# Moving a third of a depthwise convolution's taps to ScalarE and GpSimd, with all memory keys from split weights

## The chip, the cores and the metric

The kernel runs on one core of one Trainium2 chip. The metric is the device time of one execution in microseconds (us), as the median of several runs. TensorE (PE in the profile) does the matrix products, VectorE (DVE) and ScalarE (ACT) the elementwise work, GpSimd (POOL) the same at need, and SyncE (SP) issues the loads.

## The reference, cut to what matters

Two transformer blocks follow each other on 256 tokens of width 1024. The change lies in the first block. It normalises the tokens, projects them with `w_in` to queries, keys, values and the two halves of a gated convolution, runs an attention on the former and the convolution on the latter, and joins both with `w_out`. After that each token attends to a second sequence `mem` of 256 rows, which is normalised by itself and projected to keys `xk` and values `xv`.

```python
u = a * jax.nn.sigmoid(g)
u = lax.conv_general_dilated(u, conv_w.reshape(CONV_WIDTH, 1, C), ...) + conv_b
u = layernorm(u, ln_g, ln_b)
...
mn = rmsnorm(mem, norm_mem_g[l])
xk = (mn @ w_xk[l]).reshape(B, M, XATT_HEADS, XATT_HEAD_DIM)
```

The convolution is depthwise: 512 channels, 31 taps along the tokens, each channel with its own 31 weights. Everything is float32, to float32's accuracy.

## The kernel before, in words

Activations lie feature-major: a tile holds 128 features on the partitions and 256 tokens along the row. Weights come in one packed stream of blocks of 128x1024 (8 pieces of 128x128), each loaded by SP into a `raw` buffer. For the fast matrix format each block is split in two: ScalarE rounds it to a high part (`whi`, line 286) and VectorE subtracts to get the low part (`wlo`, line 287). Activations are split alike. A product of a piece is then three matmuls (`mm3`, line 484): high by high, high by low, low by high. There are four buffers each for raw, high and low blocks.

The stage that the change touches runs in this order in the program: the gate of the convolution (`ag`), the values (`v`), the queries and keys (`qk`, eight outputs from line 689) with the attention's steps between them, the keys of the memory (`xk`, lines 714 to 722), the layer norm of the convolution (726 to 750), the values of the memory (`xv`, 752), and `w_out` in two halves (line 763): half 0 takes the attention's four chunks `mh[0..3]`, half 1 the convolution's four chunks `mh[4..7]`. A scheduler turns the program's order into one fixed queue per engine: it takes what is ready by its own estimate of the times, the earlier in the program first. So an engine's queue can hold work of a later line before that of an earlier one, and once built the queue is strict.

The convolution (`conv_steps`, lines 589 to 599) keeps one sum `cacc[c]` for each of four groups of 128 channels. Tap 0 is written by ScalarE with the bias, and the taps 1 to 30 are added by VectorE, one `scalar_tensor_tensor` each (`upad` shifted, times a column of weights, plus the sum), 120 in all. `conv_hook(n)` emits n steps after a product is done.

The memory (lines 695 to 724): a `Norm` object makes from each of eight chunks a high and a low half (`parts`, line 453) and the square (`square`, line 459). The halves live in the tiles `xhi0..3` and `xlo0..3`, of which there is one buffer each, and in which the halves of the tokens lie as long as `qk` reads them. With `pe=True` the squares are summed by one float32 matmul against ones for each chunk (line 463), otherwise by VectorE adds (line 468) and one such matmul at the end (line 475). The first four outputs of `xk` are made by plain float32 matmuls from unsplit weights (`W.plain`, which holds the raw buffer until the matmuls are done) and from `mf`, a copy of the chunk times the gain, which ScalarE writes (line 702). The other four use split weights.

Of the kernel before, what the change touches and what calls it, by code (L numbers as in the profile page):

```python
# [11 lines left out]
AF = mybir.ActivationFunctionType  # L12
ALU = mybir.AluOpType
# [3 lines left out]
P = 128  # L17
T = 256
D = 1024
KD = D // P  # L20
# [11 lines left out]
CW = 31  # L32
# [271 lines left out]
def emit(tc, xT, memT, wts, params, consts, out, tap=None):  # L304
    nc = tc.nc
# [3 lines left out]
    def pool(name, bufs=1, space=None, st=None):  # L309
        kw = {} if space is None else {"space": space}  # L310
        return (st or es).enter_context(tc.tile_pool(name=name, bufs=bufs, **kw))
# [5 lines left out]
    psA = pool("psA", 3, PSUM)  # L317
# [5 lines left out]
    def nm(s):  # L323
        uid[0] += 1
        return f"{s}_{uid[0]}"

    def tl(p, shape, tag, dt=F32, bufs=None):
        kw = {} if bufs is None else {"bufs": bufs}
        return p.tile(shape, dt, tag=tag, name=nm(tag), **kw)

    def bank(which=None):
        return tl(which or psD, [P, 512], "bank")

    V, S, G, PE = nc.vector, nc.scalar, nc.gpsimd, nc.tensor

    def mm(o, l, r, start=True, stop=True, **kw):
        PE.matmul(o, l, r, start=start, stop=stop, **kw)  # L337
# [24 lines left out]
    def tt(o, a, b, op, eng=None):  # L362
        (eng or V).tensor_tensor(out=o, in0=a, in1=b, op=op)  # L363

    def stt(o, a, s, b, op0, op1):
        V.scalar_tensor_tensor(out=o, in0=a, scalar=s, in1=b, op0=op0, op1=op1)  # L366
# [16 lines left out]
    def pr(name, a=0, n=None):  # L383
        o, w = poff[name]
        return pm[:, o + a:o + (w if n is None else a + n)]
# [7 lines left out]
    W = _Stream(nc, wts, [wraw], whi, wlo)  # L393
# [4 lines left out]
    ps = bank()  # L398
# [26 lines left out]
    def both(x):  # L425
        hi = x[0]
        return bass.AP(hi.tensor, hi.offset, [list(hi.ap[0]), [1, 2 * T]])
# [56 lines left out]
    def mm3(ps, wh, wl, x, first, last):  # L484
        mm(ps, wh, x[0], first, False)
        mm(ps, wh, x[1], False, False)
        mm(ps, wl, x[0], False, last)


    def dense_s(sec, hl, nk, evac, nts, hook=None, it=None, wide=False):  # L490
        it = it or W.take(sec)
        for nt in nts:
            pw = bank(psA)
            ps = pw[:, :T]
            for k in range(nk):
                wh, wl = next(it)
                if wide:
                    mm(pw, wh, both(hl[k]), k == 0, False)
                    mm(ps, wl, hl[k][0], False, k == nk - 1)
                else:  # L500
                    mm3(ps, wh, wl, hl[k], k == 0, k == nk - 1)
            if wide:
                evac(nt, ps, pw[:, T:])
            else:
                evac(nt, ps)
            if hook:
                hook()
        return it
# [27 lines left out]
    with ExitStack() as st:  # L536
        at = pool("b1", 1, st=st)
# [17 lines left out]
        upad = [tl(at, [P, T + CW - 1], f"up{c}") for c in range(4)]  # L555
# [30 lines left out]

        cacc = [tl(at, [P, T], f"cacc{c}") for c in range(4)]

        def conv_steps():
            for c in range(4):  # L590
                a = cacc[c]
                for i in range(CW):
                    wcol = pr("cw", c * CW + i, 1)
                    src = upad[c][:, i:i + T]
                    if i == 0:
                        S.activation(a, src, AF.Identity, bias=pr("cb", c, 1), scale=wcol)
                    else:
                        stt(a, src, wcol, a, ALU.mult, ALU.add)
                    yield

        conv = conv_steps()

        def conv_hook(n=4):
            for _ in range(n):
                if next(conv, "end") == "end":
                    return

        n1.cols()
        vtok = [tl(at, [P, 512], f"vtok{t}") for t in range(2)]

        def ev_v(j, t, ps):
            S.activation(vtok[t], ps, AF.Copy, scale=n1.col(t))

        dense_m("v", n1.hl, KD, 512, ev_v, 1, lambda: conv_hook(4))
        for a, b in ((0, 1024), (1024, NC1)):
            nc.sync.dma_start(out=cs1[0][:, a:b], in_=consts[:, a:b])
# [25 lines left out]
        def att_scores(c):  # L642
            pss = [bank(), bank()]
            for q in range(2):
                for j in range(2):
                    mm(pss[j][:, q * T:(q + 1) * T], qt[c][hf[j], q * P:(q + 1) * P], kt[c][hf[j], :])
            for j in range(2):
                ps = pss[j]
                p = tl(at, [P, 2, T], "prob", bufs=4)
                mx = tl(at, [P, 4], "mx", bufs=4)  # L650
                for q in range(2):
                    ttr(p[:, q, :], ps[:, q * T:(q + 1) * T], cst("lm", q * T, T), ALU.add, ALU.min, BIG, mx[:, q:q + 1])
                for q in range(2):
                    actv(p[:, q, :], p[:, q, :], AF.Exp, bias=mx[:, q:q + 1], scale=-1.0, accum_out=mx[:, 2 + q:3 + q])
                V.reciprocal(mx[:, 2:4], mx[:, 2:4])
                for q in range(2):
                    S.activation(p[:, q, :], p[:, q, :], AF.Copy, scale=mx[:, 2 + q:3 + q])
                aps[2 * c + j] = p

        def att_turn(c):  # L660
            for kt_ in range(2):
                ps = bank()
                for j in range(2):
                    for q in range(2):
                        PE.transpose(ps[:, j * T + q * P:j * T + (q + 1) * P], aps[2 * c + j][:, q, kt_ * P:(kt_ + 1) * P], ident)
                apts[c, kt_] = tl(at, [P, 512], "pt", bufs=4)
                S.copy(apts[c, kt_], ps)

        def att_out(c):
            po = bank(psF)  # L670
            for kt_ in range(2):
                for j in range(2):
                    mm(po[hf[j], :T], vtok[kt_][:, c * P + 64 * j:c * P + 64 * j + 64], apts[c, kt_][:, j * T:(j + 1) * T],
                       kt_ == 0, kt_ == 1)
            split(po[:, :T], *mh[c])

        def att_steps():
            att_scores(0)
            yield
            for c in range(4):  # L680
                if c < 3:
                    att_scores(c + 1)
                    yield
                att_turn(c)
                att_out(c)
                yield

        itq, att = W.take("qk"), att_steps()
        for nt in range(8):
            dense_s("qk", n1.hl, KD, ev_qk, (nt,), conv_hook, it=itq)  # L690
            if nt in (1, 3, 4, 5, 6, 7):
                next(att)


        nmem = Norm(lambda c: pr("memg", c, 1), pe=True)
        mf = []
        for c in range(KD):
            mt = tl(at, [P, T], "mem", bufs=2)
            nc.sync.dma_start(out=mt, in_=memT[:, c * T:(c + 1) * T])
            nmem.chunk(c, mt)  # L700
            mf.append(tl(at, [P, T], f"mf{c}"))
            S.activation(mf[c], mt, AF.Copy, scale=pr("memg", c, 1))
        nmem.finish()
        nmem.cols()
        xk = [tl(kv, [P, T], f"xk{c}") for c in range(8)]
        xv = [tl(kv, [P, D], f"xv{t}") for t in range(2)]

        def ev_xk(nt, ps):
            tt(xk[nt], ps, nmem.rstd, ALU.mult)
# [1 line left out]
        def ev_xv(j, t, ps):  # L711
            S.activation(xv[t][:, j * 512:(j + 1) * 512], ps, AF.Copy, scale=nmem.col(t))

        itp = W.plain("xkp")
        for nt in range(4):
            ps = bank(psA)[:, :T]
            for k in range(KD):
                mm(ps, next(itp), mf[k], k == 0, k == KD - 1)
            ev_xk(nt, ps)
            next(att, None)  # L720
            conv_hook(10)
        dense_s("xk", nmem.hl, KD, ev_xk, range(4, 8), lambda: conv_hook(10))
        conv_hook(200)


        ps = bank()
# [9 lines left out]
        ps = bank()  # L736
# [31 lines left out]
    for b in range(4):  # L768
        ps = bank((psF, psD)[b // 2])
# [27 lines left out]
    with ExitStack() as st:  # L797
        at = pool("b1x", 1, st=st)
# [7 lines left out]
        for hd in range(XH):  # L806
            dense_s("xq", nx.hl, KD, ev_xq, (2 * hd, 2 * hd + 1), it=itq)
            ps = bank()
# [6 lines left out]
            p = tl(at, [P, 2, T], "prob", bufs=3)  # L815
# [30 lines left out]
    with ExitStack() as st:  # L846
        at = pool("b1m", 1, st=st)
# [39 lines left out]
    ps = bank()  # L887
# [506 lines left out]
    with ExitStack() as st:  # L1394
        at = pool("ff", 1, st=st)
# [113 lines left out]
    ps = bank(psF)  # L1509
# [22 lines left out]
    ps = bank(psF)  # L1532
# [134 lines left out]
```

## Time and profile before

| | us |
|---|---|
| median of 3 runs | 1341.27 (1338.58 to 1342.76) |
| profiled execution | 1341.65 |
| its span | 1339.9 |

The span is the time from the first to the last instruction of the one execution that was profiled; 1.75 us of its time lie around the span. Busy time of an engine counts the time in which one of its instructions runs; a pipelined successor starts a little before the record of the one in front of it ends, so the step from start to start is the price of one more instruction, and the recorded duration is an upper bound for it. A float32 matmul leaves two records. "Idle before" and the views of waits name what ended an engine's idle time. The granted clock is 1.00 at TensorE's 2.4 GHz.

### The profile page before, as it was taken

How to read it: one execution, taken by the hardware profiler on the slowest of the kernel's cores; microseconds unless marked ns; L12 is line 12 of the kernel's file. 1: busy time of each engine (PE TensorE's matmuls, PEld its weight loads, DVE VectorE, ACT ScalarE, POOL GpSimd, SP SyncE). 2: the span in 40 equal slices, each digit the busy share in tenths (PEclk: the TensorE clock that was granted, in tenths of full speed). 3: DMA queues.
4: the chain of work that ended last, by engine and by line, in shares of the span. 5: the costliest groups of instructions: out<-in, count | busy, mean ns of one | idle time of the engine just before them, and what ended most of it. 6: DMA issues, size and time to landing. Idle time of an engine off the chain costs nothing.

```text
span 1339.9 us, 22099 instructions
## 1 busy us (share of the span) xinstructions
PE 1317.6 (98%) x8095; PEld 1134.1 (85%) x8095; DVE 1059.0 (79%) x1765; ACT 871.5 (65%) x1438; POOL 75.5 (6%) x94
## 2 busy tenths in 40 slices
PE   9999999999999999999999999999999999999997
PEld 8878998888889897888888989888888788778775
DVE  7999857887668866877766886579888888887885
ACT  7663745655556847655554674668787777777774
POOL 0000000000000000022210000000101001001000
PEclk9999999999999999999999999999999999999999
DMA  8525534655554442555555444268989999999995
GB/s 291 192 83 201 169 126 136 201 188 189 189 188 150 123 131 74 172 190 188 187 184 187 158 120 138 87 204 309 373 312 377 363 378 340 358 384 332 362 394 178
DMA packets 94918, 298.27 MB, mean 223 GB/s; under 512 B 16016, under 2 KB 21456, under 8 KB 94800
## 3 DMA queue, kind: packets, MB, share of 16 engines
q1 hardware_dynamic: 92032, 291.52, 62.1%
q0 software_dynamic: 2624, 5.24, 2.0%
q8 instruction: 65, 1.06, 0.3%
q14 instruction: 53, 0.43, 0.1%
q10 hardware_dynamic: 144, 0.00, 0.0%
HBM read 289.72 MB, written 7.01 MB: 221 GB/s over the span
## 4 chain that ended last, share of the span: by engine, by line
PE 59%; issue 20%; DMA 11%; DVE 7%; ACT 2%; SPq 0%; POOL 0%; POOLq 0%; DVEq 0%; ACTq 0%
PE bank L337 58%; DMA out_dram<-yl,ix 9%; DVE wlo L287 2%; DVE cacc L366 2%; DMA raw<-in_w_dram 1%; ACT whi L286 1%; DMA pws<-dd 1%; DMA dd<-At 0%; DVE w L363 0%; DVE mid L366 0%; ACT prob L357 0%; DMA zc<-dz 0%; DVE rot L363 0%; PE bank L1127 0%; PE bank L825 0%
## 5 line engine op out<-in xcount | busy, mean ns | idle before, releaser
L287 DVE TENSOR_TENSOR wlo<-raw,whi 128x1024 fp32r<-128x1024 f32 (+1 forms) x544 | 644.4, 1210 | 153.5 <-ACT whi L286 151.0
L286 ACT CAST whi<-raw 128x1024 fp32r<-128x1024 f32 (+1 forms) x544 | 549.2, 1039 | 275.8 <-PE bank L337 159.1
L337 PE MATMUL bank<-xhi,whi 128*128 128x256 f32 (+1 forms) x864 | 240.1, 329 | 0.0
L337 PE MATMUL bank<-xlo,whi 128*128 128x256 f32 (+1 forms) x864 | 238.3, 327 | 0.4 <-DVE xlo L366 0.3
L337 PE MATMUL bank<-xhi,wlo 128*128 128x256 f32 x584 | 166.0, 284 | 1.6 <-DVE wlo L287 1.6
L337 PE MATMUL bank<-xlo,wlo 128*128 128x256 f32 x584 | 167.2, 286 | 0.0
L337 PEld LDWEIGHTS bank<-xhi,whi 128*128 128x128 f32 x864 | 146.4, 191 | 18.1 <-issue 2.4
L337 PEld LDWEIGHTS bank<-xlo,whi 128*128 128x128 f32 x864 | 145.8, 191 | 16.2 <-DVE xlo L366 0.7
L337 PE MATMUL bank<-whi,xeh 128*128 128x512 f32 x384 | 152.8, 398 | 0.0
L337 PE MATMUL bank<-whi,xel 128*128 128x512 f32 x384 | 152.0, 396 | 0.0
L337 PE MATMUL bank<-wlo,xeh 128*128 128x512 f32 x384 | 151.7, 395 | 0.0
L337 PEld LDWEIGHTS bank<-xhi,wlo 128*128 128x128 f32 x584 | 111.3, 191 | 3.0 <-DVE wlo L287 2.2
L337 PEld LDWEIGHTS bank<-xlo,wlo 128*128 128x128 f32 x584 | 111.3, 191 | 1.3 <-issue 0.7
L337 PE MATMUL bank<-whi,mid 128*128 128x512 f32 x256 | 91.0, 395 | 0.0
L337 PEld LDWEIGHTS bank<-wlo,xeh 128*128 128x128 f32 x384 | 72.0, 187 | 22.1 <-DVE wlo L287 2.2
L337 PE MATMUL bank<-u,whi 128*128 128x512 f32 x256 | 89.9, 393 | 0.0
L337 PEld LDWEIGHTS bank<-whi,xel 128*128 128x128 f32 x384 | 72.1, 188 | 16.7
L337 PEld LDWEIGHTS bank<-whi,xeh 128*128 128x128 f32 x384 | 72.1, 188 | 14.6
L337 PE MATMUL bank<-u,wlo 128*128 128x256 f32 x256 | 72.4, 283 | 0.0
L337 PE MATMUL bank<-f,whi 128*128 128x512 f32 x176 | 61.8, 393 | 0.0
L337 PEld LDWEIGHTS bank<-u,whi 128*128 128x128 f32 x256 | 48.1, 188 | 11.1
L337 PEld LDWEIGHTS bank<-whi,mid 128*128 128x128 f32 x256 | 47.5, 188 | 10.2
(397 smaller groups left out, 2113.9 us busy)
## 6 DMA issues: line engine op xcount, KB each, us to landing
raw<-in_w_dram SPq DMA_DIRECT2D x532, 512.0 KB, 4.9
raw<-in_w_dram SPq DMA_DIRECT2D x8, 384.0 KB, 3.7
raw<-in_w_dram SPq DMA_DIRECT2D x8, 256.0 KB, 4.9
dd<-At SPq DMA_DIRECT2D x6, 256.0 KB, 2.8
h<-in_x_dram SPq DMA_DIRECT2D x8, 128.0 KB, 4.8
mem<-in_mem_dram SPq DMA_DIRECT2D x8, 128.0 KB, 2.4
out_dram<-xhi POOLq DMA_DIRECT2D x4, 256.0 KB, 3.9
cs<-in_c_dram SPq DMA_DIRECT2D x1, 931.0 KB, 7.0
```

What stands on the lines that cost most here:

```text
L286: nc.scalar.copy(hi[:, s:e], raw[:, s:e])
L287: nc.vector.tensor_tensor(out=lo[:, s:e], in0=raw[:, s:e], in1=hi[:, s:e].bitcast(F32), op=ALU.subtract)
L337: PE.matmul(o, l, r, start=start, stop=stop, **kw)
L366: V.scalar_tensor_tensor(out=o, in0=a, scalar=s, in1=b, op0=op0, op1=op1)
```

## The change

VectorE keeps the sums of groups 0 and 2 and the taps 0 to 15 of group 3. All 31 taps of group 1, and the taps 16 to 30 of group 3 in a sum of their own (`chalf`), become products that ScalarE writes to a tile `tap` (six buffers) and that GpSimd adds up. VectorE adds `chalf` at the end. Each call of `conv_hook` also emits up to three of these side steps. The memory's chunks are loaded and split within the `qk` loop, with four buffers in place of two, their squares are summed by VectorE, `mf` is gone, and the first four outputs of `xk` use split weights as the others do.

```diff
+        chalf = tl(at, [P, T], "chalf")
+
+        def product(a, c, i, bias=False):
+            wcol = pr("cw", c * CW + i, 1)
+            src = upad[c][:, i:i + T]
+            if bias:
+                S.activation(a, src, AF.Identity, bias=pr("cb", c, 1), scale=wcol)
+            else:
+                S.activation(a, src, AF.Copy, scale=wcol)
+
+        def side_steps():
+            for a, c, i0 in ((cacc[1], 1, 0), (chalf, 3, 16)):
+                product(a, c, i0, c == 1)
+                for i in range(i0 + 1, CW):
+                    p = tl(at, [P, T], "tap", bufs=6)
+                    product(p, c, i)
+                    tt(a, a, p, ALU.add, G)
+                    yield
+
+        side = side_steps()
+
         def conv_steps():
-            for c in range(4):
-                a = cacc[c]
-                for i in range(CW):
-                    wcol = pr("cw", c * CW + i, 1)
-                    src = upad[c][:, i:i + T]
-                    if i == 0:
-                        S.activation(a, src, AF.Identity, bias=pr("cb", c, 1), scale=wcol)
-                    else:
-                        stt(a, src, wcol, a, ALU.mult, ALU.add)
+            for c, n in ((0, CW), (2, CW), (3, 16)):
+                product(cacc[c], c, 0, True)
+                for i in range(1, n):
+                    stt(cacc[c], upad[c][:, i:i + T], pr("cw", c * CW + i, 1), cacc[c], ALU.mult, ALU.add)
                     yield
+            for _ in side:
+                pass
+            tt(cacc[3], cacc[3], chalf, ALU.add)
...
             for _ in range(n):
                 if next(conv, "end") == "end":
                     return
+            for _ in range(3):
+                next(side, None)
...
+        nmem = Norm(lambda c: pr("memg", c, 1))
         itq, att = W.take("qk"), att_steps()
         for nt in range(8):
             dense_s("qk", n1.hl, KD, ev_qk, (nt,), conv_hook, it=itq)
             if nt in (1, 3, 4, 5, 6, 7):
                 next(att)
-        nmem = Norm(lambda c: pr("memg", c, 1), pe=True)
-        mf = []
-        for c in range(KD):
-            mt = tl(at, [P, T], "mem", bufs=2)
-            nc.sync.dma_start(out=mt, in_=memT[:, c * T:(c + 1) * T])
-            nmem.chunk(c, mt)
-            mf.append(tl(at, [P, T], f"mf{c}"))
-            S.activation(mf[c], mt, AF.Copy, scale=pr("memg", c, 1))
+            if 2 <= nt < 6:
+                for c in (2 * nt - 4, 2 * nt - 3):
+                    mt = tl(at, [P, T], "mem", bufs=4)
+                    nc.sync.dma_start(out=mt, in_=memT[:, c * T:(c + 1) * T])
+                    nmem.chunk(c, mt)
...
-        itp = W.plain("xkp")
-        for nt in range(4):
-            ps = bank(psA)[:, :T]
-            for k in range(KD):
-                mm(ps, next(itp), mf[k], k == 0, k == KD - 1)
-            ev_xk(nt, ps)
+        def xk_hook():
             next(att, None)
-            conv_hook(10)
-        dense_s("xk", nmem.hl, KD, ev_xk, range(4, 8), lambda: conv_hook(10))
+            conv_hook(6)
+
+        dense_s("xkp", nmem.hl, KD, ev_xk, range(4), xk_hook)
+        dense_s("xk", nmem.hl, KD, ev_xk, range(4, 8), xk_hook)
         conv_hook(200)
```

## Rows read from the trace of the kernel before

**Rows 1.** The page's first part: busy time of each engine over the span.
```profile
PE 1317.6 (98%) x8095; PEld 1134.1 (85%) x8095; DVE 1059.0 (79%) x1765; ACT 871.5 (65%) x1438; POOL 75.5 (6%) x94
```

**Rows 2.** Busy time by stretch; columns: length, PE, PEld, DVE, ACT, POOL, PE clock, DMA, GB/s.
```profile
24.50:74.50 50.00, 49.27 (x357) 43.98 (x355) 49.05 (x132) 31.90 (x67) 2.08 (x2) 1.00 0.59 203
74.50:110.00 35.50, 34.07 (x206) 27.84 (x202) 33.88 (x89) 22.12 (x48) 0.00 (x0) 1.00 0.38 126
110.00:136.00 26.00, 23.63 (x106) 19.07 (x104) 24.16 (x41) 8.70 (x10) 0.00 (x0) 0.93 0.58 191
136.00:154.00 18.00, 18.00 (x125) 16.82 (x126) 13.98 (x26) 13.57 (x24) 0.00 (x0) 1.00 0.42 138
...
150.00:420.00 270.00, 269.34 (x1643) 240.48 (x1642) 196.18 (x337) 148.47 (x258) 1.39 (x8) 1.00 0.54 175
```

**Rows 3.** What PE waited for between 15 and 200 us: total, times, longest.
```profile
PE bank L337 <- DVE wlo L287: 1.6, 2, 0.8
PE bank L337 <- DVE cacc L366: 1.2, 1, 1.2
```

**Rows 4.** Busy time by stretch, as above, of the split keys and the stretch behind the waits.
```profile
100.00:109.90 9.90, 9.90 (x80) 9.77 (x79) 9.40 (x21) 5.47 (x6) 0.00 (x0) 1.00 0.64 212
114.50:118.70 4.20, 4.20 (x22) 4.20 (x23) 2.99 (x4) 0.00 (x0) 0.00 (x0) 0.59 0.58 192
```

**Rows 5.** The timeline of PE around 96 to 100 us: start, length of the merged piece.
```profile
96.40 4.15 PE L337 MATMUL bank<-mf,raw 128*128 128x256 f32 x18
100.20 0.47 PE L337 MATMUL bank<-xhi,whi 128*128 128x256 f32 x1
```

**Rows 6.** Groups of instructions between 15 and 150 us, on PE: busy, mean ns, idle before.
```profile
L337 PE MATMUL bank<-mf,raw 128*128 128x256 f32 x64 | 15.9, 382 | 0.6 <-ACT mf L702 0.6
L337 PE MATMUL bank<-sq,ones 128*128 128x256 f32 x16 | 5.0, 403 | 0.5 <-ACT sq L461 0.5
```

**Rows 7.** The timeline of DVE between 107 and 115 us.
```profile
107.73 2.85 DVE L366 SCALAR_TENSOR_TENSOR cacc<-up,pm,cacc 128x256 f32<-128x256 f32 x7
110.50 0.42 DVE L363 TENSOR_TENSOR xk<-bank,rstd 128x256 f32<-128x256 f32 x1
...
113.20 1.22 DVE L287 TENSOR_TENSOR wlo<-raw,whi 128x1024 fp32r<-128x1024 f32 x1
114.34 0.48 DVE L366 SCALAR_TENSOR_TENSOR cacc<-up,pm,cacc 128x256 f32<-128x256 f32 x1
```

**Rows 8.** Groups of instructions between 24.5 and 136 us, on ACT.
```profile
L286 ACT CAST whi<-raw 128x1024 fp32r<-128x1024 f32 x26 | 27.3, 1049 | 30.5 <-DMA raw<-in_w_dram 15.2 <-PE bank L337 12.7 <-DVE cacc L366 1.7
...
L702 ACT ACTIVATE mf<-mem,pm 128x256 f32<-128x256 f32 x8 | 4.0, 494 | 0.0
```

**Rows 9.** GpSimd's adds elsewhere in this kernel: ns min/median/max, first and last start.
```profile
L363 POOL TENSOR_TENSOR fg<-fg,rstd x22: 733/1464/1470, 562.3 to 680.9; 128x256 f32<-128x256 f32 x22
```

**Rows 10.** The timeline of DVE, and that of POOL, around 50 us.
```profile
49.98 0.63 DVE L363 TENSOR_TENSOR rot<-rot,cs 128x256 f32<-128x256 f32 x1
...
50.94 0.41 DVE L363 TENSOR_TENSOR kt<-rot,rot 128x256 f32<-128x256 f32 x1
...
49.50 0.84 POOL L757 CAST br<-brf 128x786 fp32r<-128x786 f32 x1 [4.05 <-DMA brf<-in_c_dram]
```

**Rows 11.** One group of DVE (ns min/median/max), and the POOL copies beside its last three.
```profile
L363 DVE TENSOR_TENSOR X<-mid,eg x6: 277/280/767, 493.0 to 824.0; 128x128 f32<-128x128 f32 x6
...
822.04 1.70 POOL L1280 COPY Xf<-Xt 64x768 f32<-64x768 f32 x2 [79.15 <-ACT Xt L1273]
```

**Rows 12.** `w_out`: its inputs' last halves, and its products on PE (first and last start).
```profile
L337 PE MATMUL bank<-mh,whi x128: 281/282/285, 142.2 to 165.0; 128*128 128x256 f32 x128
...
L363 DVE TENSOR_TENSOR mh<-rot,mh x4: 418/421/426, 144.7 to 150.3; 128x256 fp32r<-128x256 f32 x4
```

**Rows 13.** The memory's chunks: ACT's timeline at 79 us, and SP's own waits.
```profile
79.45 0.51 ACT L456 ACTIVATE xhi<-mem,pm 128x256 fp32r<-128x256 f32 x1 [4.19 <-DMA mem<-in_mem_dram]
...
SPq L699 <- DVE xhi L366: 14.5, 3, 11.5
```

## The prediction

> **What bounds the kernel now.** I read the busy table first: PE is busy for 1317.6 of 1339.9 us [rows 1], so only what shortens PE's queue, or what PE waits for, can count. Then the stretches. The change lies between 24.5 and 154 us, and there two engines are full, not one: over the first three stretches PE is busy for 49.27 + 34.07 + 23.63 = 107.0 us of 111.5, and DVE for 49.05 + 33.88 + 24.16 = 107.1 [rows 2]. ACT has room: 31.90 + 22.12 + 8.70 = 62.7. The row for 150 to 420 us shows PE busy for 269.34 of 270, so a shift at 154 us should be carried to the end, and none is made good there.
>
> The waits show how DVE reaches PE: twice a low half of weights came late (1.6 us), once a convolution sum (1.2) [rows 3]. After them the granted clock fell to a mean of 0.59 for 4.2 us, between the levels of 1.2 and 2.4 GHz [rows 4]. Set against full clock that is 4.2 x 0.41 = 1.7 us.
>
> **The change, part by part. PE.** The plain keys are 32 matmuls of two records, 64, and the squares 16 records [rows 6]. Eighteen such records take 100.20 - 96.40 = 3.80 us, 0.211 each [rows 5]; the mean duration of 0.38 is pipelined and isn't the price. So 80 x 0.211 = 16.9 us go. In come 32 x 3 = 96 split matmuls at 9.90 / 80 = 0.124 us [rows 4], 11.9 us, and one float32 matmul on the summed squares, 2 x 0.211 = 0.4. PE's balance: 16.9 - 11.9 - 0.4 = **4.6 us less**.
>
> **DVE.** There were 4 x 30 = 120 taps, and 30 + 30 + 15 = 75 stay; 45 go. Seven taps take 110.50 - 107.73 = 2.77 us, 0.396 each [rows 7]: 17.8 us less. In come four more low halves, at 114.34 - 113.20 = 1.14 us [rows 7], 4.6 us, and seven adds of squares and one of `chalf`, at 0.42 as a 128x256 operation of two tensors has it [rows 7], 3.4 us. Without more, DVE has 17.8 - 8.0 = 9.8 us less.
>
> **GpSimd and what it costs DVE.** GpSimd adds 30 + 14 = 44 products. Its adds of this shape take 0.733 us at best and 1.464 in the median [rows 9], 32 to 64 us in all; from some 26 us on they end by 90, far before the sums are needed. What matters is what they do to VectorE. At 49.50 GpSimd reads a tile for 0.84 us, and a VectorE operation with two SBUF inputs that starts at 49.98 takes 0.63 us, where the same shape takes 0.41 at 50.94: 0.22 more [rows 10]. Beside the copies at 822 us one of six equal operations takes 0.767 against 0.280, 0.49 more [rows 11]. Taps and low halves have two SBUF inputs too. No row shows an add of GpSimd beside taps, so I bound it: nothing for each add (it falls beside an operation that reads PSUM, or into a gap), up to its own shortest duration of 0.733, 44 x 0.733 = 32 us. A gain is excluded, as nothing in it shortens a VectorE operation. I take 0.22, the collision in this very stretch with an operation of this size: 44 x 0.22 = 9.7 us. DVE's balance is then 9.7 - 9.8, **nothing**.
>
> The Trainium skill (SBUF — State Buffer, Who interferes with whom) says that a VectorE instruction with two SBUF inputs and a GpSimd instruction that reads SBUF exclude each other for the whole instruction, and the later one waits. The collisions agree in kind. Taken for every add at full length it would make the upper bound's 32 us, and by the reckoning of the third rival below a time of 1361.
>
> **ACT.** 45 more products, each at most 0.494 us as the equal write of `mf` [rows 8]: 22.2; four more high parts at 1.049, 4.2; the eight `mf` go, 4.0. Sum 22.4 more, 85 of 111.5 us: it fits into the idle time, most of which ACT spent waiting for loads (15.2) and for free buffers (12.7) [rows 8]. But the products wait for one of six `tap` buffers, which GpSimd frees, and behind a waiting product the casts of weights queue, for which DVE and PE wait (a rival, below).
>
> **The memory's loads and halves.** Eight loads move ahead in SP's queue, past the loads of weights for the rest of `qk` and for `xk`; four buffers in place of two let four go early. The halves themselves can't: each of their tiles is the one in which the tokens' halves lie until `qk` has read them, near 74 us. So the other four loads still wait for a chunk to be split; before, SP waited 14.5 us for that in three waits, and ACT 4.19 us for one landing [rows 13]. Until then `mf`, with buffers of its own, kept PE fed; now PE has the first chunks' products of three outputs (three banks), 3 x 4 x 3 x 0.124 = 4.5 us, and the attention's steps. I cost it at nothing; without that cover it is up to the 4.2 us of that landing.
>
> **The stalls.** PE was idle for 0.73 + 1.43 + 2.37 us in the three stretches [rows 2], and lost 1.7 to the clock. The plain weights held all four raw buffers until their matmuls were done; split, they free them at once, so the loads behind them, for which ACT waited 15.2 us, come earlier. With DVE as full as before I take half of the third stretch's loss, (2.37 + 1.7) / 2 = 2.0 us.
>
> **Sum**, against the profiled execution: 1341.65 - 4.6 - 2.0 = **1335 us**. That execution lies 0.4 us above the median of the runs, which I leave inside the rounding.
>
> **The rivals.** *All of it comes through.* GpSimd's adds cost DVE nearly nothing, it gains the 9.8 us, and the stalls vanish: 1341.65 - 4.6 - (0.73 + 1.43 + 2.37 + 1.7) = 1331. For it: the median of GpSimd's adds is twice the best [rows 9], as if it were GpSimd that waits, and not VectorE. Against: both collisions above.
>
> *Nothing is left.* PE's 4.6 us go into the wait for the memory's halves (up to 4.2), and the stall at 110 us finds its like: 1341. For it: the single buffers. Against: four chunks instead of two can be ready.
>
> *Slower, by the collisions.* At 0.5 us for each add, as beside the copies [rows 11], DVE loses 22 us and has 22 - 9.8 = 12.2 more. The convolution's halves come that much later. The last of them was there at 150.3 + 0.4 = 150.7 us; `w_out` runs from 142.2 to 165.2, so half 1 begins halfway, at 153.7 [rows 12]. With 3.0 us of room the end moves by 12.2 - 3.0 = 9.2: 1351. It decides where an add costs more than (9.8 + 3.0) / 44 = 0.29 us, between the two collisions read.
>
> By the Trainium skill's rule cited above this rival is the expected one, since most of DVE's work here has two SBUF inputs; only the row at 50 us gives it a smaller price.
>
> *Slower, by ACT's queue.* If the order of ACT is laid out for adds of 0.733 us and they take 1.464, GpSimd ends 44 x 0.73 = 32 us late. Six buffers hold 6 x 1.464 = 8.8 us of it and four split blocks 4 x 8 x 3 x 0.124 = 11.9; 11.5 reach PE: 1353. Against: three side steps for each hook need 4.4 us of GpSimd, and a `qk` output has 24 split matmuls, 3.0 us, and the attention's steps, so the pace asked for is near the one to be had.
>
> **How the numbers follow.** Forecast 0.38, all of it 0.08, nothing left 0.22, collisions 0.24, ACT's queue 0.08. A measurement can tell 0.3%, 4 us, from no change. Faster: the first two less a little, 0.44; the same, with that, 0.24; slower 0.24 + 0.08 = 0.32. The range goes from 1329 (the forecast with all of the stalls and a little of the clock elsewhere) to 1351, the collisions' price; above lies ACT's queue and the costlier half of the collisions. The likeliest sign alone would be 1329 to 1338.
>
> **What would show it.** Right: between 74 and 110 us PE does the same work in some 5 us less; the adds take 0.7 to 1.5 us; the taps beside them show 0.6 to 0.7 us now and then, their sum over the median about 10 us; PE's waits for low halves around 110 us shrink. Wrong: taps with a mean over 0.8 us beside the adds, a wait of PE for the convolution's halves behind half 0 of `w_out`, casts of ACT that wait for GpSimd, or PE idle for more than 2 us at 74 to 80 us.

## The result, and the profile after

The change makes the kernel slower: 1352.78 us in the median (1351.40 to 1355.45), against 1341.97 for the kernel before on the same chip, a ratio of 1.0091 with a 95% interval of 1.0080 to 1.0103. The forecast was 1335, with 1351 as the upper end. The profiled execution of after has a span of 1352.4 us.

First the stretches, as in [rows 2]: busy time of PE, PEld, DVE, ACT and POOL, PE's granted clock, share and rate of DMA.

```profile
24.50:74.50 50.00, 38.62 (x238) 34.43 (x237) 49.18 (x80) 35.86 (x72) 35.53 (x35) 0.86 0.53 183
74.50:110.00 35.50, 30.82 (x215) 24.98 (x215) 34.46 (x96) 30.62 (x76) 11.26 (x12) 0.90 0.35 109
110.00:136.00 26.00, 23.78 (x170) 22.00 (x168) 25.48 (x51) 9.10 (x12) 0.00 (x0) 1.00 0.42 139
136.00:154.00 18.00, 18.00 (x80) 14.62 (x79) 12.30 (x22) 13.40 (x20) 0.00 (x0) 1.00 0.55 181
```

DVE is as full as before in the first stretch (49.18 against 49.05) but gets through 80 operations, not 132, and PE through 238 records, not 357. PE is idle there for 11.4 us instead of 0.7. Over the four rows it is idle for 18.3 us instead of 4.5, 13.7 more, and the clock granted in the first two falls to a mean of 0.86 and 0.90 of 2.4 GHz, where it was 1.00. In the last row it is full, as before: nothing is made good.

What PE waited for between 15 and 160 us, the three longest, and the timeline at three of these waits:

```profile
PE bank L337 <- DVE kt L363: 11.1, 2, 7.7
PE bank L337 <- DVE gate L363: 3.6, 1, 3.6
PE bank L337 <- DVE wlo L287: 3.0, 2, 2.2
```

```profile
36.02 1.22 PE L337 MATMUL bank<-whi,xhi 128*128 128x512 f32 x2 [3.63 <-DVE gate L363]
...
63.73 2.08 PE L337 MATMUL bank<-kt,qt 64*128 64x256 f32 x8 [7.75 <-DVE kt L363]
...
94.39 2.08 PE L337 MATMUL bank<-kt,qt 64*128 64x256 f32 x8 [3.38 <-DVE kt L363]
```

Neither the convolution's end nor a half of it is in the list. PE waits for the gate, which frees a bank, and for the rotated keys, which the attention needs. Both are VectorE's, and both come late because of what stands ahead of them in its queue. This is its timeline as GpSimd starts adding, at 25.79:

```profile
25.07 0.48 DVE L366 SCALAR_TENSOR_TENSOR cacc<-up,pm,cacc 128x256 f32<-128x256 f32 x1
25.47 1.22 DVE L287 TENSOR_TENSOR wlo<-raw,whi 128x1024 fp32r<-128x1024 f32 x1
26.61 0.96 DVE L366 SCALAR_TENSOR_TENSOR cacc<-up,pm,cacc 128x256 f32<-128x256 f32 x1
27.49 1.76 DVE L287 TENSOR_TENSOR wlo<-raw,whi 128x1024 fp32r<-128x1024 f32 x1
29.18 0.96 DVE L366 SCALAR_TENSOR_TENSOR cacc<-up,pm,cacc 128x256 f32<-128x256 f32 x1
...
25.79 10.10 POOL L363 TENSOR_TENSOR cacc<-cacc,tap 128x256 f32<-128x256 f32 x9 [5.25 <-ACT tap L598]
```

Before the first add a tap takes 0.48 us and a low half 1.22, as in [rows 7]. From 26.61 on the tap takes 0.96 and the low half 1.76, 0.48 and 0.54 more. The groups between 24.5 and 111 us give the sum; first two groups of before, then four of after (two of DVE, and GpSimd's, from 15 us on):

```profile
L366 DVE SCALAR_TENSOR_TENSOR cacc<-up,pm,cacc 128x256 f32<-128x256 f32 x95 | 40.8, 479 | 0.0
L287 DVE TENSOR_TENSOR wlo<-raw,whi 128x1024 fp32r<-128x1024 f32 x17 | 20.6, 1218 | 1.1 <-ACT whi L286 1.1
```

```profile
L366 DVE SCALAR_TENSOR_TENSOR cacc<-up,pm,cacc 128x256 f32<-128x256 f32 x46 | 30.0, 665 | 0.0
L287 DVE TENSOR_TENSOR wlo<-raw,whi 128x1024 fp32r<-128x1024 f32 x18 | 25.6, 1424 | 0.0
...
L363 POOL TENSOR_TENSOR cacc<-cacc,tap 128x256 f32<-128x256 f32 x30 | 30.0, 999 | 11.8 <-ACT tap L598 10.1
L363 POOL TENSOR_TENSOR chalf<-chalf,tap 128x256 f32<-128x256 f32 x14 | 14.9, 1066 | 27.4 <-ACT tap L598 26.6
```

The taps are longer by 46 x 0.186 = 8.6 us, the low halves by 18 x 0.206 = 3.7; smaller groups with two SBUF inputs (rotation tables, rotations, sums of squares, the memory's halves, the gated inputs) add some 5 by their own means. That is 17 us, or 0.39 for each of the 44 adds. With 45 taps fewer, 17.8 us, and the 8.0 us of new work that the prediction counts, VectorE so has some 7 us more to do than before. The groups that read a bank kept their time, 0.404 us against 0.408 for the rotation's product with a bank.

The consequence can be followed through the stage. The last key was rotated at 76.9 us before; PE could score from there. After, and `w_out` after:

```profile
L363 DVE TENSOR_TENSOR kt<-rot,rot x4: 414/417/937, 62.7 to 93.9; 128x256 f32<-128x256 f32 x4
...
L363 DVE TENSOR_TENSOR mh<-rot,mh x4: 416/418/419, 141.3 to 147.5; 128x256 fp32r<-128x256 f32 x4
...
L337 PE MATMUL bank<-mh,whi x128: 279/282/284, 154.9 to 177.6; 128*128 128x256 f32 x128
```

The last key is 17.0 us later, `w_out` 12.7 us (154.9 against 142.2 [rows 12]). The convolution's last half starts at 147.5, earlier than the 150.3 of before, and PE doesn't wait for it. The convolution is done sooner (its last tap starts at 128.7 us, against 135.4), but that isn't what the end hangs on. PE is idle for 13.7 us more and by the prediction's sum has 4.6 less to do, so some 3.6 of the 12.7 us are left for the lower granted clock: an estimate, as no run measured the clock's part.

### The profile page after: what moved, and what is told of

Its sections match the earlier page's. It is cut to its first block, busy times and chain, and to the rows that moved or that the text cites. A ratio compares the mean times of both kernels' runs of the same rounds, so it can differ in the third digit from the quotient of the medians.

```text
span 1352.4 us, 22236 instructions
## 1 busy us (share of the span) xinstructions
PE 1316.7 (97%) x8113; PEld 1135.2 (84%) x8113; DVE 1065.7 (79%) x1732; ACT 890.1 (66%) x1479; POOL 119.2 (9%) x138
## 4 chain that ended last, share of the span: by engine, by line
PE 80%; DVE 8%; issue 6%; DMA 4%; ACT 1%; POOL 0%; SPq 0%; POOLq 0%; DVEq 0%; ACTq 0%
PE bank L337 78%; DMA out_dram<-yl,ix 2%; DVE cacc L366 2%; DVE wlo L287 2%; ACT whi L286 1%; PE bank L1637 1%; DMA dd<-At 1%; DMA pws<-dd 1%; DVE rot L363 0%; DVE w L363 0%; DMA raw<-in_w_dram 0%; DVE mid L366 0%; DMA zc<-dz 0%; DVE rot L654 0%; PE bank L1143 0%
## 5 line engine op out<-in xcount | busy, mean ns | idle before, releaser
L287 DVE TENSOR_TENSOR wlo<-raw,whi 128x1024 fp32r<-128x1024 f32 (+2 forms) x548 | 652.9, 1216 | 162.2 <-ACT whi L286 159.9
L286 ACT CAST whi<-raw 128x1024 fp32r<-128x1024 f32 (+2 forms) x548 | 553.3, 1040 | 279.7 <-PE bank L337 170.8
L337 PE MATMUL bank<-xhi,whi 128*128 128x256 f32 (+1 forms) x896 | 246.3, 328 | 0.0
L337 PE MATMUL bank<-xlo,whi 128*128 128x256 f32 (+1 forms) x896 | 245.1, 326 | 0.4 <-DVE xlo L366 0.3
L337 PE MATMUL bank<-xhi,wlo 128*128 128x256 f32 x600 | 170.8, 285 | 3.0 <-DVE wlo L287 3.0
L337 PE MATMUL bank<-xlo,wlo 128*128 128x256 f32 x600 | 171.7, 286 | 0.0
L337 PEld LDWEIGHTS bank<-xhi,whi 128*128 128x128 f32 x896 | 151.5, 191 | 17.9 <-issue 2.1
L337 PEld LDWEIGHTS bank<-xlo,whi 128*128 128x128 f32 x896 | 151.1, 191 | 16.9 <-issue 1.2
L337 PEld LDWEIGHTS bank<-xhi,wlo 128*128 128x128 f32 x600 | 114.5, 191 | 4.7 <-DVE wlo L287 3.6
L1652 POOL DMA_INDIRECT out_dram<-yl,ix x16 | 28.6, 1787 | 410.0 <-ACT yl L1651 371.5
```

The costliest lines, as they stand in the source:

```text
L286: nc.scalar.copy(hi[:, s:e], raw[:, s:e])
L287: nc.vector.tensor_tensor(out=lo[:, s:e], in0=raw[:, s:e], in1=hi[:, s:e].bitcast(F32), op=ALU.subtract)
L1652: G.indirect_dma_start(out=out[:, :], out_offset=bass.IndirectOffsetOnAxis(ap=ix[:, i:i + 1], axis=0), in_=y, in_offset=None, element_offs ...
```

## The experiments

All ratios are against the kernel before on the same chip, with 95% intervals. The start of `w_out` in the profile (before: 142.2, after: 154.9) shows how far a run's stage came; a stretch of full PE follows it in most.

**Collisions alone.** The kernel before, with 44 adds on GpSimd that nothing uses:

```
+        scr = tl(at, [P, T], "scr")
+        G.memset(scr, 0.0)
+        for _ in range(44):
+            tt(scr, scr, upad[1][:, :T], ALU.add, G)
         conv = conv_steps()
```

> The kernel before with 44 more GpSimd adds of 128x256 that read a scratch tile and one padded convolution input, which no other instruction waits for; the queues of PE, DVE, ACT and SP are the same, instruction by instruction. Collisions theory: a GpSimd add that meets a VectorE operation with two SBUF inputs costs it some 0.48 us (taps of 0.96 against 0.48 us in the changed kernel), three of four adds meet one, so DVE loses 44 x 0.75 x 0.48 = 16 us, taps of 0.96 us appear, and the time is 8 to 16 us over before: 1350 to 1358. Order theory (the loss comes from the new order of the queues, not from collisions): 1342 within 2, taps at 0.48 us throughout.

1360.62 us, 1.0152 (1.0134 to 1.0170), `w_out` from 161.6. The queues of PE, DVE, ACT and SP are those of before, instruction by instruction. Groups as above:

```profile
L366 DVE SCALAR_TENSOR_TENSOR cacc<-up,pm,cacc 128x256 f32<-128x256 f32 x64 | 38.3, 640 | 0.0
L287 DVE TENSOR_TENSOR wlo<-raw,whi 128x1024 fp32r<-128x1024 f32 x13 | 20.6, 1589 | 0.0
...
L363 POOL TENSOR_TENSOR scr<-scr,up 128x256 f32<-128x256 f32 x44 | 44.2, 1005 | 5.7 <-DVE up L366 2.4
```

Adds that nobody waits for cost 20 us, so it is no dependency. The taps' excess is 64 x 0.161 = 10.3 us, that of the low halves 13 x 0.371 = 4.8, and the smaller groups with two SBUF inputs have 4.6 more: some 20 us, as much as the time.

**The same time on GpSimd without reading.** The adds replaced by fills of about their length:

```
+        scr = tl(at, [P, 3 * T], "scr")
+        G.tensor_copy(scr[:, :T], upad[1][:, :T])
+        for _ in range(44):
+            G.memset(scr, 0.0)
```

> The same with 44 GpSimd fills of 128x768, which only write, in place of the adds; about 0.74 us each, so GpSimd is as long busy. Collisions theory, by reads: 1342 within 2, no tap longer than 0.52 us. If any work of GpSimd blocks VectorE, whether it reads or not: as the run with 44 adds, 1350 to 1358. Order theory: 1342 within 2.

1342.15 us, 1.0011 (1.0000 to 1.0023).

```profile
L366 DVE SCALAR_TENSOR_TENSOR cacc<-up,pm,cacc 128x256 f32<-128x256 f32 x98 | 41.9, 476 | 0.0
...
L604 POOL MEMSET scr<- 128x768 f32 x44 | 32.6, 742 | 2.4
```

A GpSimd busy for 32.6 us costs nothing when it only writes; what the fills lack beside the adds is the reading of SBUF, and the arithmetic.

The Trainium skill (SBUF — State Buffer, Who interferes with whom) names this pair, a VectorE instruction with two SBUF inputs and a GpSimd instruction that reads, and spares the one that only writes. Both runs agree.

**The changed kernel with narrow adds.** The same 44 adds over 32 of 256 columns; it leaves out the other columns' side products. Its queues are nearly those of after.

```
-                    tt(a, a, p, ALU.add, G)
+                    tt(a[:, :32], a[:, :32], p[:, :32], ALU.add, G)
```

> The changed kernel with each GpSimd add over 32 of the 256 columns; left out are the products' other 224 columns in the sums of group 1 and of chalf. The order of the queues differs from the changed kernel's in a dozen places at most. Collisions theory: an add now holds VectorE for at most 0.1 us, so DVE gets back some 13 of 17 us, the waits for kt and gate vanish, and the time falls to 1331 to 1340, below before. Order theory: it stays within 3 us of the changed kernel, 1350 to 1356.

1339.53 us, 0.9997 (0.9986 to 1.0008), `w_out` from 140.2. Against after that is some 13 us less by the ratios, and in this run all of VectorE's operations have their time of before within 1 us in sum, where after had 17 more: the collisions are the loss. But without them the change is only level with before. Stretches and waits of this run:

```profile
24.50:74.50 50.00, 48.51 (x348) 43.38 (x347) 49.16 (x128) 48.68 (x108) 19.78 (x45) 1.00 0.59 205
74.50:110.00 35.50, 29.49 (x210) 24.62 (x209) 33.92 (x84) 21.12 (x45) 1.41 (x1) 0.94 0.32 104
```

```profile
PE bank L337 <- DVE wlo L287: 4.1, 3, 2.2
PE bank L337 <- DVE kt L363: 3.0, 3, 1.8
```

PE is idle for 6.0 us in the second row, where it was 1.4. That is 4.6 us more, as much as the split keys were to save.

**The memory's part alone**, with the convolution of before (ten taps behind each of the memory's blocks):

```
-        nmem = Norm(lambda c: pr("memg", c, 1), pe=True)
+        nmem = Norm(lambda c: pr("memg", c, 1))
...
-                mm(ps, next(itp), mf[k], k == 0, k == KD - 1)
...
+        dense_s("xkp", nmem.hl, KD, ev_xk, range(4), xk_hook)
```

> The kernel before with the memory's part of the change alone: all keys from split weights, squares summed by adds, chunks loaded within the queries' loop with four buffers; all 120 taps stay on VectorE and GpSimd adds nothing. Collisions theory: PE has 4.6 us less, DVE 8.0 us more, which is full here, so between 1339 and 1347 and no stall above 3 us before the attention's scores. Memory theory (the single buffers of the halves make the loss): 1348 or more, with PE idle at 74 to 95 us.

1349.07 us, 1.0053 (1.0040 to 1.0067), `w_out` from 148.5.

```profile
PE bank L337 <- DVE wlo L287: 6.8, 4, 4.9
```

The part that was to save PE 4.6 us costs 7 by itself, by the ratio; I had expected 1347 at most. The four low halves and seven sums of squares put 7.5 us on a VectorE that is full, and PE then waits for low halves, up to 4.9 us at a time. The time lies in the range of the rival, in which the single buffers of the halves make the loss. But the last of the halves is there at 78.9 us, and the longest wait ends at 104.0, for a low half of weights that stood behind eleven taps in VectorE's queue.

**The convolution's part alone**, with the memory of before. For want of SBUF its products have three buffers, not six, and `chalf` lies where `ahalf` lay.

```
+        chalf = tl(at, [P, T], "ahalf", bufs=2)
...
+                    p = tl(at, [P, T], "tap", bufs=3)
```

> The convolution's part of the change alone (44 products on ScalarE, their adds on GpSimd, 45 taps fewer on VectorE), with the memory's part of before. Collision theory: VectorE saves 45 x 0.396 = 17.8 us and pays about 35 collisions of 0.48 us = 16.8, so its balance is near nothing and so is the time: 1338 to 1346, taps mean about 0.66 us, and the two parts of the change add up to the whole (this one about +2, the memory's part +7 as measured). Rival, ScalarE's queue waits for GpSimd's adds: over 1350, with waits of ScalarE for the accumulators of several us. Rival, the memory's part carries the whole loss: 1330 or less.

1356.28 us, 1.0107 (1.0092 to 1.0123), `w_out` from 154.9: 14 us slower than before, where I expected nothing. Its taps have a mean of 0.601 and its low halves of 1.504 between 24.5 and 111 us, so the collisions are there; ScalarE also waits 7.2 us in all for GpSimd to free a product's buffer, against 1.2 us in after, which is what this run's rival had named:

```profile
ACT tap L598 <- POOL cacc L363: 4.5, 5, 1.3
...
ACT tap L598 <- POOL ahalf L363: 2.7, 6, 1.2
```

So this run isn't the convolution's part as after has it, and the parts don't add up: 14 and 7 alone, 11 to 12 together. How much of the 14 the three buffers make wasn't separated.

**Running sums in PSUM.** A tap then has one SBUF input. VectorE's three sums take one bank, from a pool that loses one of two until the convolution is done; the last tap writes to SBUF.

```
-    psF = pool("psF", 2, PSUM)
+    psC = pool("psC", 1, PSUM, st=stF)
+    psF = pool("psF1", 1, PSUM, st=stF)
...
+                a = pacc[c]
...
+                    stt(cacc[c] if i == n - 1 else a, upad[c][:, i:i + T], pr("cw", c * CW + i, 1), a, ALU.mult, ALU.add)
```

> The changed kernel with VectorE's three running sums kept in PSUM until their last tap, so that a tap reads one SBUF operand and one PSUM operand; GpSimd's 44 adds stay as they are. In the trace of after, VectorE's operations that read PSUM kept their time beside the adds (0.41 us). Theory that a collision needs two SBUF operands on VectorE: taps fall from a mean of 0.66 to 0.40 to 0.52 us in the stretch with the adds, and the time to 1338 to 1346, near the 1339.5 of the narrow adds. Rival, any VectorE operation waits for GpSimd's reads, or the loss is not in the taps: taps stay at 0.6 us or more and the time at 1350 to 1356.

1342.98 us, 1.0008 (0.9998 to 1.0018): some 11 us under after by the ratios, with the same adds emitted in the same places.

```profile
L287 DVE TENSOR_TENSOR wlo<-raw,whi 128x1024 fp32r<-128x1024 f32 x22 | 29.6, 1346 | 0.0
L368 DVE SCALAR_TENSOR_TENSOR bank<-up,pm,bank 128x256 f32<-128x256 f32 x48 | 22.9, 478 | 0.0
```

The taps are back at 0.478 beside 30 + 14 adds; the low halves, whose inputs both stay in SBUF, still take 1.346. So the collision hangs on VectorE's second SBUF input, operation by operation.

The same with the memory of before (three buffers again), and in the kernel before with no GpSimd work:

> The convolution's part alone, with VectorE's running sums in PSUM. If the collisions ate what the convolution's part saves and PSUM operands avoid them, VectorE is 13 to 18 us lighter before w_out, the memory's part of before keeps PE's cover, and the time is 1324 to 1336, under both kernels. If PE is the limit once VectorE is lighter (the stretch of 110 to 136 us of before has PE busy 0.9): 1334 to 1341. Rival, PSUM does not help: as the convolution's part alone, 1338 to 1346.

> The kernel before with its four running sums in PSUM and nothing else: the price of such a tap beside no GpSimd work. Theory: a tap with one PSUM operand and a PSUM result takes 0.40 to 0.50 us as one in SBUF (0.477), and the time is that of before within 5 us: 1336 to 1346. Rival, PSUM taps are longer by 0.1 us or more: 124 x 0.1 = 12 us more on VectorE, 1345 to 1355, and the two runs above carry that too.

The first: 1347.81, 1.0045 (1.0032 to 1.0059), so 8.5 us under its twin in SBUF, but over before and over all that I had given for it. The second: 1354.71, 1.0085 (1.0070 to 1.0101), 12 us up by one wait:

```profile
PE bank L339 <- DVE cacc L368: 15.1, 2, 14.3
```

```profile
139.43 11.57 DVE L368 SCALAR_TENSOR_TENSOR bank<-up,pm,bank 128x256 f32<-128x256 f32 x22
151.04 0.48 DVE L368 SCALAR_TENSOR_TENSOR cacc<-up,pm,bank 128x256 f32<-128x256 f32 x1
```

The mean record of such a tap is 0.483 us, as in SBUF, but the record isn't the price: from start to start these 22 take (151.04 - 139.43) / 22 = 0.53 us each, where seven in SBUF took 0.396 [rows 7]. Followed by another kind of operation a PSUM tap takes 0.39, so the added 0.13 falls on taps straight behind one another, 60 of the 120 here: some 8 us. In this the rival, a longer PSUM tap, was right, and 1354.71 lies in its range. The order adds to it: with the sums in one bank the scheduler laid fewer taps early (66 by 111 us against 95), 26 were left at 136, and `w_out` waited for the convolution. Why it laid them so I didn't settle. It shows that the convolution's end does bound the time once it is late enough, as my rival had it.

**Does the place of the adds matter?** Late adds (emitted only behind the memory's eight blocks) and early relief (two taps instead of four behind the early blocks, eight instead of six behind the memory's):

```
-            for _ in range(3):
+            for _ in range(m):
                 next(side, None)
...
-            conv_hook(6)
+            conv_hook(6, 6)
```

with `conv_hook(n=4, m=0)` as the default, and, for the second, `conv_hook(n=2, m=3)` as the default and `conv_hook(8, 3)` behind the memory's blocks.

> The changed kernel with the same 44 products and adds, all of them emitted in the memory's eight blocks (six a block) and none in the value and query-key blocks. Place theory: the loss of after came because the adds lie beside the query-key blocks, where VectorE sets PE's pace and has as many taps as before, while the 45 taps saved lie after 110 us; put beside the memory's blocks, the collisions fall where the taps are fewer. First stretch 24.5 to 74.5 us with PE busy over 47 us and taps at 0.48, w_out from 141 to 149 us, time 1340 to 1349. Sum theory: VectorE's total alone counts, and about 35 collisions of 0.48 us cost the same wherever they lie: 1350 to 1355.

> The changed kernel with two taps instead of four behind each value and query-key block and eight instead of six behind each of the memory's, the adds where they were. Place theory: 9 blocks x 2 taps x 0.48 to 0.96 us leave the stretch in which PE waits for VectorE (kt, gate), and go to where the convolution's halves had some 7 us of room before w_out: 1342 to 1348, waits for kt and gate under 8 us together (14.7 in after). Sum theory: 1350 to 1355, the waits only moved.

1353.40, 1.0099 (1.0080 to 1.0118), and 1354.24, 1.0107 (1.0090 to 1.0124): as after. In the second PE's waits for gate and keys fall from 14.7 to 10.1 us and those for low halves rise from 3.0 to 6.2: they only moved. The first didn't test the place. GpSimd's operations at line 363 in the first run:

```profile
24.50:74.50 50.00, 30.45 (x32) 0.86 0.52 184
```

The scheduler takes an add when its inputs are ready by its estimate, wherever it was emitted, so 32 still lay there. The next run, otherwise as the first, holds them by a dependency: the side's tap weights are copied with a bias of zero times the last key.

```
+        S.activation(zero, kt[3][:, :1], AF.Copy, scale=0.0)
+        S.activation(cwl, pr("cw"), AF.Identity, bias=zero)
```

> The changed kernel with the side's tap weights read from a copy that is made only after the last key block, so that no product or add can lie beside the query-key blocks (in the run with late adds they still did: 32 of them before 74.5 us). Place theory: first stretch with PE over 47.5 of 50 us and taps at 0.48; the 44 adds from about 80 us on cost VectorE up to 0.48 us each, in a stretch where it has 45 taps fewer; w_out from 141 to 149 us and 1340 to 1349 us. Sum theory, VectorE's total before w_out counts alone: 1350 to 1355.

1355.16, 1.0106 (1.0087 to 1.0126).

```profile
24.50:74.50 50.00, 48.70 (x353) 43.68 (x353) 49.52 (x135) 34.06 (x71) 3.01 (x2) 1.00 0.59 209
74.50:110.00 35.50, 21.29 (x145) 17.66 (x142) 34.05 (x61) 28.83 (x68) 21.20 (x26) 0.84 0.19 65
110.00:136.00 26.00, 20.70 (x121) 18.71 (x121) 23.73 (x32) 15.72 (x26) 16.04 (x19) 0.89 0.33 115
```

```profile
PE bank L337 <- DVE wlo L287: 12.7, 5, 4.9
PE bank L337 <- ACT whi L286: 5.9, 2, 5.6
```

The first stretch is that of before, and the whole loss comes in the next two, now as waits for halves of weights. The move didn't pay: VectorE is nearly as full in these rows (34.05 of 35.5 us, 23.73 of 26) as in the first. But the hold also crowds ScalarE, as PE's 5.9 us for high halves show, so this run alone doesn't say which of the two made the loss (the last run below bears on it).

**Looking for a version that wins.** The version with sums in PSUM, three taps and two adds behind an early block, seven and four behind one of the memory's; the same with one memory chunk behind each of the eight query-key blocks; the same as the first with all of groups 1 and 3 on the side (60 adds); and the PSUM version with held adds:

```
-            for a, c, i0 in ((cacc[1], 1, 0), (chalf, 3, 16)):
+            for a, c, i0 in ((cacc[1], 1, 0), (cacc[3], 3, 0)):
...
-            for c, n in ((0, CW), (2, CW), (3, 16)):
+            for c, n in ((0, CW), (2, CW)):
```

> Running sums in PSUM (no collision at the taps) with three taps and two adds a block early, seven and four in the memory's blocks. If what the PSUM version still lost early is VectorE's and ScalarE's load there (PE waited 3.7 us for kt and 5.0 for pt): 1334 to 1341. If it is the memory's halves, which nothing here moves: 1341 to 1345.

> The run before it with the memory's halves and squares one chunk behind each of the eight query-key blocks, not two behind each of the middle four. If the bunched halves and the first low weight halves cause PE's idle time at 74 to 84 us: 1 to 4 us less than the run before it, 1331 to 1339. If not: within 1.5 us of it.

> The version with running sums in PSUM, three taps and two adds a block early, with all 31 taps of two chunks on ScalarE and GpSimd (60 adds) and VectorE's taps down to 60. In that version VectorE ended the convolution last (PE waited 3.3 us for it before w_out). If VectorE's total is the limit: 16 taps x 0.48 = 7.7 us less on it, w_out with no wait, 1334 to 1339, under both kernels. If ScalarE (45 of 50 us busy early) or GpSimd becomes late: 1341 to 1350, with waits for pt, whi or cacc on GpSimd.

> The version with running sums in PSUM (four taps a block early, as after) and the side's adds held until after the last key block. Place theory: the splits' collisions (wlo 1.35 us beside adds, 1.22 without) leave the query-key blocks, PE there as before (over 48.5 of 50 us), 1335 to 1341. Rival, GpSimd's 44 adds of 0.8 to 1.0 us then end the convolution (80 + 44 us = 124 to 130 us, still ahead of w_out) but ScalarE's products crowd the low halves: 1341 to 1346.

In this order: 1340.90, 1.0002 (0.9988 to 1.0015); 1343.21, 1.0028 (1.0009 to 1.0047); 1340.40, 0.9993 (0.9981 to 1.0006); 1353.98, 1.0094 (1.0075 to 1.0113). The spread run didn't test the bunching of the memory's halves: VectorE writes them from 76.3 to 87.5 us, against 77.1 to 86.2 in the run before it, since their tiles come free no sooner. None beats the kernel before. The nearest, with 60 adds, has `w_out` from 139.0 and these stretches:

```profile
24.50:74.50 50.00, 45.81 (x315) 41.01 (x314) 49.19 (x105) 45.38 (x96) 41.59 (x42) 0.97 0.58 206
74.50:110.00 35.50, 33.94 (x249) 28.98 (x248) 32.47 (x80) 31.34 (x73) 17.79 (x21) 1.00 0.33 110
110.00:136.00 26.00, 26.00 (x132) 22.07 (x131) 21.17 (x36) 13.63 (x20) 0.42 (x1) 1.00 0.65 214
```

What PE gains against before in the third row (26.00 us busy against 23.63), where VectorE has gaps at last, it has lost in the first (45.81 against 49.27).

The last of the four, with PSUM sums and held adds, shows what the hold costs without collisions:

```profile
74.50:110.00 35.50, 25.63 (x164) 20.78 (x165) 26.54 (x61) 28.60 (x68) 20.35 (x25) 0.81 0.25 80
...
PE bank L339 <- ACT whi L286: 6.4, 2, 6.0
...
ACT tap L602 <- POOL cacc L365: 6.5, 18, 1.1
```

VectorE is idle for 9.0 us in this row and its operations are hardly longer than before (1 us in sum), yet the time is that of the held run in SBUF. PE waits for high halves: ScalarE's products come all at once, wait for GpSimd's buffers, and the casts of weights stand behind them. So the held runs don't decide on the place of the collisions.

## Why the prediction was wrong

**The price of an add: the step that failed.** I took 0.22 us, from one row at 50 us [rows 10], and it measured 0.39 on average over 44 adds, 17 us where the sum had 9.7. The row I chose was nearest in time and size, but it showed one partial overlap: GpSimd's cast had 0.36 us left when VectorE's operation began. The other row [rows 11] had 0.49, and a tap that meets an add pays 0.48. The point of decision that I had worked out, 0.29, lies under 0.39: the rival that I gave 0.24 was the case in its cause. The bound of 0.733 for each add was far off: an operation that meets an add pays 0.48 to 0.54, some adds meet none, and GpSimd's adds wait as well (1.0 us beside VectorE against 0.733 at best in [rows 9]). Those 22 adds, which I took as a sign for GpSimd waiting instead of VectorE, could not give the price: 21 of them start 0.36 us behind a low half that runs already (567.39 and 567.75 us, for one). The low half keeps its 1.23 us and the add takes 1.46, so there the add came second and paid alone. Beside the full queue of after both pay.

By the rule of the Trainium skill (SBUF — State Buffer, Who interferes with whom) that rival was the expected one, as the prediction said; it was right in sign, and its full price for every add, 1361, was too much for the 44 adds of this kernel.

**The balance of VectorE: 9.8 us that were not to be had.** Weighing 17.8 us saved against 8.0 and the collisions took every microsecond of VectorE as worth the same. The run with narrow adds has the saving without the collisions, and came out level. Where the 45 taps lay is the likely reason; taps of before up to the last key, and from there to the first of the memory's keys, and then PE's busy time on products of `mf` in the same two:

```profile
24.50:77.30 52.80, 18.16 (x41) 1.00 0.56 193
77.30:94.10 16.80, 12.52 (x30) 1.00 0.15 47
...
24.50:77.30 52.80, 1.45 (x7) 1.00 0.56 193
77.30:94.10 16.80, 10.06 (x41) 1.00 0.15 47
```

In after the same two spans, 24.5 to 94.3 and 94.3 to 103.6 us, hold 35 and 4 taps; in the run with narrow adds (to 78.0 and 87.8 us) it is 34 and 5. So 26 of the 45 went out of a span in which PE was fed for 10 of 16.8 us by plain products that need nothing of VectorE; only 6 went out of the one in which PE waits for it. And with PE idle for only 4.5 us in four stretches before, and 1.7 us lost to the clock, no saving of VectorE could give more than that; an added load has no such limit.

**The memory's halves, "cost at nothing".** Wrong by about as much as PE's 4.6 us, and in another way than the bound of 4.2 us foresaw: not a landing, but low halves of weights (6.8 us alone, 4.1 with narrow adds) and keys that are late. The plain products were cover for VectorE, not only for the loads: in the run with the memory's part alone 2 taps are left between the last key and the first of the memory's, where it was 30. My rival "nothing is left" had the size of this and named the wrong wait.

**PE's balance and the stalls.** The 4.6 us on PE were not measured by themselves, as they never reached the end; the 2.0 us of stalls didn't come, since PE is idle for 2.2 us in the third stretch as for 2.4 before.

**The place.** In my rival the convolution's halves are late for half 1 of `w_out`. They are early. The collisions reach PE 60 to 120 us sooner, at the gate and at the keys, through VectorE's strict queue. That is why the 3.0 us of room at `w_out` weren't there to soften them. So the 1351 of that rival is near the measured 1352.78 by luck: with the measured 17 us in place of 22 its own sum gives 1341.65 + 17 - 9.8 - 3.0 = 1346.

**ACT's queue.** As expected it fits. ScalarE waits for GpSimd's buffers for 1.2 us in all, in three waits; the rival of 1353 had the time almost to the microsecond and the wrong cause, by luck (its mechanism shows in the held runs):

```profile
ACT tap L598 <- POOL cacc L363: 1.2, 3, 0.5
```

**What stays open:** why the version with PSUM sums and no GpSimd work has its taps laid late, how much three buffers cost the convolution's part alone, whether the collisions would cost less at another place, and what the lower clock has of the loss.

## What to carry to other kernels

Before work goes to GpSimd, look at VectorE's operations beside it: if they have two SBUF inputs and VectorE sets the pace, each add that is taken over costs what a tap saves (0.39 and 0.396 us here), and what VectorE saves comes back only where another engine waits for it. Where such operations can have one input in PSUM, the collision goes, at 0.13 us for each that stands straight behind another; a control with work that nobody uses, once reading and once only writing, prices it in two runs. And when two engines are both full, count a saving on one of them only up to the other's idle time, but an added load in full.

## What the runs showed of the hardware

A tap meeting an add took 0.94 to 0.96 us instead of 0.47 to 0.48, and in after only 3 of 75 lay between. The add pays too: 1.02 us in the mean in after and 1.005 beside the kernel before, against 0.733 at best. VectorE's taps with one PSUM input and a PSUM result took 0.478 to 0.483, as those in SBUF do (0.475 to 0.479), but straight behind one another they start 0.53 us apart, not 0.396. A fill of 128 x 768 on GpSimd, 0.742 us each, left taps at 0.476. After PE's waits the granted clock was down for long: a mean of 0.50 at 95 to 100 us of after, the level of 1.2 GHz, behind the wait of 3.4 us for keys that ended at 94.4.

```profile
95.00:100.00 5.00, 5.00 (x22) 3.21 (x19) 5.00 (x18) 5.00 (x14) 0.00 (x0) 0.50 0.00 0
```
